# Hybrid Conformer/RWKV-7 trunk on one core: the scheduler's queue order taken from a simulated timeline

## Chip, cores, metric

The kernel runs on one core of one Trainium2 chip. The metric is device time in microseconds of one execution; lower is better. The engines named below are PE (matrix multiply), DVE (vector), ACT (scalar), POOL, and SP, whose queue issues most of the DMAs. Each engine works through its own queue in the order in which the built program lists it.

## Reference

A decoder trunk of 2 layers over 512 tokens of width 1024, with 16 learned tokens put in front (528 rows). All of it is float32. Each layer is: half a SwiGLU feed-forward step, a mixer, half a SwiGLU step, each added to the residual and layer-normalised.

```python
for l in range(DEPTH):
    h = layer_norm(ALPHA*h + 0.5*swiglu(h, ffn1_wg, ffn1_wu, ffn1_wd))
    h = layer_norm(ALPHA*h + mixer(h))
    h = layer_norm(ALPHA*h + 0.5*swiglu(h, ffn2_wg, ffn2_wu, ffn2_wd))

def mixer(x):
    z = x @ w_in                      # glu_a, glu_b, r/k/v and low-rank inputs, two gates
    yc = conv_branch(glu_a, glu_b)    # gated, 31-tap depthwise causal convolution, norm, silu, @ wo
    yr = rwkv_branch(zr)              # time mix, then a scan over tokens per head, group norm, @ wo
    return (sigmoid(gate_c)*yc + sigmoid(gate_r)*yr) @ w_out

def scan_step(S, r, w, k, v, kk, a):  # S is 64x64 for each of 16 heads
    sa = S @ -kk
    S = S*w + outer(sa, kk*a) + outer(v, k)
    return S, S @ r
```

## The kernel before

A float32 product is made of three products of reduced-precision float32 parts: the weight is split into `w_hi` (a cast on ACT, L121 and L123) and `w_lo` (a subtraction on DVE, L132), the activation into a high and a low part (`xh`, `xl`). `wunit` loads a weight tile through SP (L112) and splits it; raw tiles and split tiles have two buffers each in the mixer. Tokens are columns, handled as two halves of 264 (256 in parts of the last layer).

In the feed-forward steps and at the end of a mixer PE streams such products (L185). The mixer is different. Its scan is turned into chunks of 64 tokens, for four groups of four heads (q = 0 to 3):

- `prep(q)` projects k, r and v of a group (token mixing on ACT and DVE, L702 and L704), normalises k (L875, a chain of small DVE operations, L887) and makes the decayed forms.
- `scores(q)`: for each of 8 chunks PE transposes (L986) and multiplies (L995), DVE masks (L1003, L1005), ACT copies; the strictly lower blocks go to DRAM.
- `inverse(q)`: the blocks come back with 16x16 blocks on partitions, and `substitution` solves them in 15 dependent steps of a product (L1028) and a sum (L1032) on DVE. Groups 0 to 2 do it in two lots, so 60 instructions; group 3 in one, 30. The result goes through DRAM into `dd`, and PE joins the blocks (L1074, then three rounds of L1085 with copies between).
- `scan(q)`: 8 chunks, each depending on the last. PE transposes v (L1155), multiplies the state (L1160), ACT copies; PE (L1168, L1170), ACT copies; PE updates the state (L1177), DVE adds and scales it (L1180, L1181), and L1185 makes the output. A step of this sequence is called a link below.
- `post(q)`: group norm of the outputs (L1213 to L1234) and L1279 to L1287.

Work without a place in that chain is called fill. On PE it is the projections of `proj` (L203): 48 matmuls for a 128-column tile, for the two halves of the gated convolution input, the two gates, and k, r and v of later groups. On DVE it is the 31-tap convolution: 30 instructions of L814 for each of 8 tiles, traced at an offset of 4000 towards low priority. The loop interleaves the scan of a group with the scores of the next one, which are traced 50 lower:

```python
for q in range(4):
    scores = self.scores(q + 1, N) if q < 3 else iter(())
    for c, _ in enumerate(self.scan(q, Q)):
        with self.tc.high_priority(offset=-SC_LATE):
            next(scores, None)
        ...
    if q < 3:
        self.inverse(q + 1, N)
    post = early or self.post(q, Q)
    filler(FILL[3][q])
    Q, N = N, prep(q + 2, FILL[4][q]) if q < 2 else None
```

The traced order is only the priority. What stands in a queue is decided when the context closes: a scheduler keeps a clock for each engine, and gives a free engine the instruction of highest priority that its clock says is ready. So the time that the scheduler believes an instruction takes decides how much fill lands between two links. Only `schedule_with_timeline_sim` below is touched; no kernel code says how much fill stands where.

## Time and profile before

| | |
|---|---|
| median of 3 runs | 3326.89 us (3325.49 to 3332.04) |
| profiled execution: its own time | 3317.26 us |
| profiled execution: span of its instructions | 3315.6 us |
| PE busy | 3174.3 us, 96% |
| DVE busy | 1955.1 us, 59% |
| ACT busy | 1228.6 us, 37% |
| mean granted PE clock | 0.952 |

PE executes 27172 matmuls. Busy time of an engine is the time in which it had an instruction at work; the granted clock is 1.00 where PE runs at full rate and 0.50 where the throttle halves it, in which case a busy PE does half as much. The four feed-forward steps take most of the span; the two mixers, without the layer norms ahead of them and the products behind them, lie at 443 to 1125 us and 2101 to 2766 us.

### The profile page before, as it was taken

The page shows a single profiled execution, that of the slowest core. Times are in us where ns is not written, and L with a number is a line of the kernel's source. Part 1 is how long each engine was busy: PE and PEld are TensorE (multiplying, and loading weights), DVE is VectorE, ACT ScalarE, POOL GpSimd, SP SyncE. Part 2 cuts the span into 40 slices and gives each one's busy share as a digit, 9 for nine tenths or more (in the row PEclk, how much of TensorE's full clock was granted, in tenths as well). Part 3 has the DMA queues.
Part 4 walks back from the last instruction along what each step waited for, and adds up shares of the span by engine and source line. Part 5 has one row for each costly group of instructions (what it writes and reads, how often), then busy time and mean ns, then how long its engine had stood idle before and what let it go on. Part 6 is the DMA issues. An engine that isn't in the chain of part 4 may idle for free. (4 is left out here: it accounts for less than half of the span.)

```text
span 3315.6 us, 65004 instructions
## 1 busy us (share of the span) xinstructions
PE 3174.3 (96%) x27172; PEld 3047.5 (92%) x27172; DVE 1955.1 (59%) x4183; ACT 1228.6 (37%) x2477; POOL 19.7 (1%) x89
## 2 busy tenths in 40 slices
PE   9999989899999899999999999889999998999998
PEld 8999979789889899999999999788888898999997
DVE  4343449687788876343363434586688878663434
ACT  4232244334353454322242322534343444342322
POOL 0000000000000000000000000000000000000000
PEclk9999969799899999999999999898898999999999
DMA  5232234222333542332232322432233435432321
GB/s 152 72 107 80 80 113 120 77 75 72 93 106 101 181 135 78 89 109 82 79 96 72 107 82 78 145 97 75 68 96 90 115 89 180 137 90 78 109 82 52
DMA packets 569012, 326.48 MB, mean 98 GB/s; under 512 B 83148, under 2 KB 535104, under 8 KB 568718
## 3 DMA queue, kind: packets, MB, share of 16 engines
q1 hardware_dynamic: 563726, 312.74, 32.8%
q10 hardware_dynamic: 4608, 8.52, 0.7%
q8 instruction: 213, 3.49, 0.4%
q0 software_dynamic: 384, 1.07, 0.1%
q14 instruction: 81, 0.66, 0.1%
HBM read 270.81 MB, written 47.12 MB: 96 GB/s over the span
## 5 line engine op out<-in xcount | busy, mean ns | idle before, releaser
L185 PE MATMUL mm<-xh,w_hi 128*128 128x264 f32 (+1 forms) x2880 | 819.9, 286 | 16.6 <-ACT xh L395 15.8
L185 PE MATMUL mm<-xh,w_lo 128*128 128x264 f32 (+1 forms) x2880 | 821.4, 285 | 0.5 <-DVE w_lo L132 0.5
L185 PE MATMUL mm<-xl,w_hi 128*128 128x264 f32 (+1 forms) x2880 | 819.4, 285 | 0.3 <-DVE xl L396 0.2
L132 DVE TENSOR_TENSOR w_lo<-w_raw,w_hi 128x1024 fp32r<-128x1024 f32 (+3 forms) x540 | 535.0, 993 | 457.8 <-ACT w_hi L123 394.0
L123 ACT CAST w_hi<-w_raw 128x1024 fp32r<-128x1024 f32 (+2 forms) x388 | 372.3, 961 | 770.3 <-PE mm L185 540.1
L185 PEld LDWEIGHTS mm<-xh,w_hi 128*128 128x128 f32 x2880 | 546.4, 190 | 19.7 <-ACT xh L395 17.7
L185 PEld LDWEIGHTS mm<-xh,w_lo 128*128 128x128 f32 x2880 | 547.6, 190 | 0.8 <-DVE w_lo L132 0.8
L185 PEld LDWEIGHTS mm<-xl,w_hi 128*128 128x128 f32 x2880 | 547.1, 190 | 1.2 <-DVE xl L396 1.1
L203 PE MATMUL mm<-xh,w_hi 128*128 128x264 f32 x1760 | 400.2, 305 | 46.8 <-DVE glus L794 17.9
L203 PE MATMUL mm<-xh,w_lo 128*128 128x264 f32 x1760 | 395.7, 304 | 6.6 <-DVE w_lo L132 6.6
L185 PE MATMUL mm<-hl,w_hi 128*128 128x264 f32 (+1 forms) x1408 | 400.5, 284 | 0.0
L185 PE MATMUL mm<-hh,w_hi 128*128 128x264 f32 (+1 forms) x1408 | 400.3, 284 | 0.0
L185 PE MATMUL mm<-hh,w_lo 128*128 128x264 f32 (+1 forms) x1408 | 398.7, 283 | 0.0
L203 PE MATMUL mm<-xl,w_hi 128*128 128x264 f32 x1760 | 397.7, 304 | 0.0
L814 DVE SCALAR_TENSOR_TENSOR cacc<-cu,cw,cacc 128x528 f32<-128x528 f32 (+1 forms) x480 | 362.3, 755 | 9.3 <-ACT cacc L812 2.1
L203 PEld LDWEIGHTS mm<-xh,w_hi 128*128 128x128 f32 x1760 | 297.4, 202 | 55.7 <-issue 30.3
L203 PEld LDWEIGHTS mm<-xh,w_lo 128*128 128x128 f32 x1760 | 293.7, 201 | 13.3 <-DVE w_lo L132 7.1
L203 PEld LDWEIGHTS mm<-xl,w_hi 128*128 128x128 f32 x1760 | 294.9, 201 | 6.9
L443 DVE TENSOR_TENSOR g<-g,mm 128x264 f32<-128x264 f32 (+1 forms) x176 | 74.7, 427 | 330.1 <-PE mm L185 318.4
L185 PEld LDWEIGHTS mm<-hh,w_lo 128*128 128x128 f32 x1408 | 265.1, 188 | 0.1
L185 PEld LDWEIGHTS mm<-hl,w_hi 128*128 128x128 f32 x1408 | 264.9, 188 | 0.2
L185 PEld LDWEIGHTS mm<-hh,w_hi 128*128 128x128 f32 x1408 | 264.6, 188 | 0.1
(340 smaller groups left out, 4517.2 us busy)
## 6 DMA issues: line engine op xcount, KB each, us to landing
w_raw<-in_w_in_dram SPq DMA_DIRECT2D x116, 512.0 KB
w_raw<-in_ffn_wg_dram SPq DMA_DIRECT2D x88, 512.0 KB
w_raw<-in_ffn_wu_dram SPq DMA_DIRECT2D x88, 512.0 KB
w_raw<-in_ffn_wd_dram SPq DMA_DIRECT2D x64, 384.0 KB
w_raw<-in_ffn_wd_dram SPq DMA_DIRECT2D x64, 320.0 KB
w_raw<-in_rwkv_wo_dram SPq DMA_DIRECT2D x16, 512.0 KB
w_raw<-in_conv_wo_dram SPq DMA_DIRECT2D x16, 512.0 KB
w_raw<-in_w_out_dram SPq DMA_DIRECT2D x16, 512.0 KB
```

The lines of the kernel that those rows point to most:

```text
L123: self.nc.scalar.copy(hi[:, :kt], raw[:, :kt])
L132: self.nc.vector.tensor_tensor(lo[:, k], raw[:, k], hi[:, k].bitcast(F32), op=ALU.subtract)
L185: self.nc.tensor.matmul(pm, a[:, k, :], b[:, xk + k, s], start=first and k == 0 and j == 0, stop=last and k == nk - 1 and j == 2)
L203: nc.tensor.matmul(pm[:, h, :n], a[:, wk + k, :], b[:, xk + k, s:s + n], start=first and k == 0 and j == 0, stop=last and k == nk - 1 and ...
L443: nc.vector.tensor_tensor(g, g, ps[1][:, :n], op=ALU.mult)
L814: tap = nc.vector.scalar_tensor_tensor(y, x, w, y, op0=ALU.mult, op1=ALU.add)
```

## The change

The scheduler takes its estimates from a simulated timeline of the machine; before, it used a fixed figure for each instruction.

```diff
-    with tile.TileContext(nc) as tc, ExitStack() as ctx:
+    with tile.TileContext(nc, schedule_with_timeline_sim=True) as tc, ExitStack() as ctx:
         Trunk(ctx, tc, aps, out).run()
```

The same instructions are built, apart from waits: PE has 24276 matrix instructions in both, DVE 4183. ACT has 35 loads of its function tables where it had 31. In the middle of the feed-forward steps the order is the same on all engines; around layer norms a few instructions change places; in the two mixers fill and chain are interleaved in another way. Three places show it.

PE, scan of group 2 in layer 0, between the multiplication of the state (L1160) and the next link (L1168). `sv` is the state, `G` and `FB` the decayed rows, `w` and `va` ACT's copies; L203 is fill. Before:

```order
L1185 MATMUL ch<-va,sb 64x64 x4
L1160 MATMUL tr<-sv,G 64x64 x4
L203 MATMUL mm<-xl,w_hi 128x264 x2
L203 MATMUL mm<-xh,w_lo 128x264
L986 MATMUL sc<-ident,FB 128x128
L1168 MATMUL tr<-w_10566,G 64x64
```

Now:

```order
L1185 MATMUL ch<-va,sb 64x64 x4
L1160 MATMUL tr<-sv,G 64x64 x4
L995 MATMUL sc<-G,FB 128x128 x4
L203 MATMUL mm<-xh,w_hi 128x264
L203 MATMUL mm<-xl,w_hi 128x264 x2
L203 MATMUL mm<-xh,w_lo 128x264 x2
L203 MATMUL mm<-xh,w_hi 128x264 x2
L203 MATMUL mm<-xl,w_hi 128x264 x2
L203 MATMUL mm<-xh,w_lo 128x264 x2
L203 MATMUL mm<-xh,w_hi 128x264 x2
L203 MATMUL mm<-xl,w_hi 128x264 x2
L1168 MATMUL tr<-w_10566,G 64x64
```

Three fill matmuls stood in this link; now 15 do, and in most links of scans 0, 1 and 2 that have fill it is 20 to 25.

PE, scan of group 3 in layer 0, the same link. Before:

```order
L1185 MATMUL ch<-va,sb 64x64 x4
L203 MATMUL mm<-xh,w_lo 128x264 x2
L203 MATMUL mm<-xh,w_hi 128x264 x2
L203 MATMUL mm<-xl,w_hi 128x264
L1160 MATMUL tr<-sv,G 64x64 x4
L203 MATMUL mm<-xl,w_hi 128x264
L203 MATMUL mm<-xh,w_lo 128x264 x2
L203 MATMUL mm<-xh,w_hi 128x264 x2
L1168 MATMUL tr<-w_11598,G 64x64
```

Now:

```order
L1185 MATMUL ch<-va,sb 64x64 x4
L1160 MATMUL tr<-sv,G 64x64 x4
L1168 MATMUL tr<-w_11598,G 64x64
L1170 MATMUL ch<-sv,G 64x64
```

All fill has moved out of this scan, to places ahead of it.

DVE, substitution of group 1 in layer 0. `ix` is the block being solved, `is` a product, `cacc` the convolution's sum. Before:

```order
L1028 TENSOR_TENSOR is<-im,ix 64x55 x2
L1032 TENSOR_TENSOR ix<-ix,is 64x11x5 x2
L1028 TENSOR_TENSOR is<-im,ix 64x60 x2
L1032 TENSOR_TENSOR ix<-ix,is 64x10x6 x2
L1028 TENSOR_TENSOR is<-im,ix 64x63 x2
L1032 TENSOR_TENSOR ix<-ix,is 64x9x7 x2
```

Now:

```order
L1028 TENSOR_TENSOR is<-im,ix 64x55
L814 SCALAR_TENSOR_TENSOR cacc<-cu_4629,cw,cacc 128x528
L1028 TENSOR_TENSOR is<-im,ix 64x55
L1032 TENSOR_TENSOR ix<-ix,is 64x11x5
L814 SCALAR_TENSOR_TENSOR cacc<-cu_4629,cw,cacc 128x528
L1032 TENSOR_TENSOR ix<-ix,is 64x11x5
L1028 TENSOR_TENSOR is<-im,ix 64x60
L814 SCALAR_TENSOR_TENSOR cacc<-cu_4629,cw,cacc 128x528
L1028 TENSOR_TENSOR is<-im,ix 64x60
L1032 TENSOR_TENSOR ix<-ix,is 64x10x6
```

A tap of the convolution now stands between nearly all of these steps.

Counted over the queues of layer 0 between marks of the chain (layer 1 is alike), the fill matmuls L203 on PE and the taps L814 on DVE are:

| Stretch of the mixer (marks on PE) | fill before | fill now | taps before | taps now |
|---|---|---|---|---|
| start: low-rank products to first L986 of scores 0 | 350 | 402 | 22 | 31 |
| scores 0: to their last L995 | 112 | 270 | 8 | 29 |
| substitution 0: to first L1074 | 189 | 0 | 18 | 0 |
| inverse 0 and prep: to first L986 of scores 1 | 119 | 151 | 12 | 4 |
| scan 0 with scores 1: to last L995 | 54 | 360 | 11 | 56 |
| substitution 1 (and the end of scan 0) | 240 | 113 | 19 | 30 |
| inverse 1 and prep: to first L986 of scores 2 | 287 | 127 | 17 | 3 |
| scan 1 with scores 2 | 94 | 257 | 12 | 57 |
| substitution 2 (and the end of scan 1) | 210 | 192 | 11 | 15 |
| inverse 2 and prep: to first L986 of scores 3 | 260 | 126 | 26 | 0 |
| scan 2 with scores 3 | 86 | 575 | 12 | 0 |
| substitution 3 (and the end of scan 2) | 275 | 19 | 30 | 0 |
| inverse 3: to first L1160 of scan 3 | 55 | 0 | 16 | 0 |
| scan 3 | 161 | 0 | 11 | 0 |
| end of the scan to the products behind the mixer | 100 | 0 | 15 | 15 |

## Prediction

> **What bounds the kernel now.** I read the page first, then busy time by stretch, then single waits. The page:
>
> ```profile
> span 3315.6 us, 65004 instructions
> PE 3174.3 (96%) x27172; PEld 3047.5 (92%) x27172; DVE 1955.1 (59%) x4183; ACT 1228.6 (37%) x2477; POOL 19.7 (1%) x89
> PEclk9999969799899999999999999898898999999999
> ```
>
> PE is busy nearly always; only 141 us could be won by closing its waits. The clock dips where the mixers lie. So I cut the first mixer at the marks of its chain (columns: stretch, its length, then busy time of PE, its weight loads, DVE, ACT and POOL, granted clock, DMA share, GB/s); the rows stand in the order of the front table, with the two mixers whole and a feed-forward stretch after them.
>
> ```profile
> 443.00:541.10 98.10, 92.78 (x556) 85.48 (x556) 56.02 (x113) 42.90 (x76) 0.30 (x4) 0.76 0.47 154
> 541.10:564.70 23.60, 23.41 (x199) 20.68 (x199) 22.77 (x75) 12.01 (x33) 0.00 (x0) 1.00 0.48 132
> 564.70:605.50 40.80, 30.47 (x236) 28.83 (x232) 35.44 (x96) 9.28 (x15) 0.85 (x4) 0.87 0.33 77
> 605.50:657.70 52.20, 47.42 (x468) 44.03 (x468) 31.19 (x74) 20.22 (x56) 0.30 (x4) 0.74 0.21 61
> 657.70:697.70 40.00, 39.73 (x464) 32.33 (x462) 28.56 (x90) 23.17 (x69) 0.44 (x2) 1.00 0.18 51
> 697.70:739.20 41.50, 35.23 (x262) 34.55 (x258) 35.64 (x100) 8.09 (x16) 0.42 (x2) 0.88 0.38 93
> 739.20:801.60 62.40, 62.40 (x624) 60.45 (x623) 41.99 (x98) 25.21 (x65) 0.30 (x4) 0.89 0.31 93
> 801.60:849.90 48.30, 48.09 (x503) 38.24 (x499) 37.47 (x128) 27.77 (x76) 0.44 (x2) 1.00 0.30 83
> 849.90:885.10 35.20, 31.05 (x254) 29.84 (x253) 29.77 (x91) 10.40 (x22) 0.42 (x2) 0.95 0.39 100
> 885.10:948.70 63.60, 63.59 (x618) 60.57 (x619) 48.98 (x108) 24.73 (x64) 0.16 (x2) 0.87 0.34 94
> 948.70:992.30 43.60, 43.54 (x471) 35.48 (x469) 34.65 (x123) 25.18 (x71) 0.44 (x2) 1.00 0.34 94
> 992.30:1029.70 37.40, 37.40 (x319) 36.47 (x317) 34.58 (x80) 12.62 (x24) 0.00 (x0) 1.00 0.56 151
> 1029.70:1054.00 24.30, 24.30 (x314) 23.73 (x313) 16.96 (x26) 9.69 (x34) 0.00 (x0) 0.80 0.31 95
> 1054.00:1101.50 47.50, 47.50 (x503) 40.68 (x503) 33.91 (x106) 22.95 (x56) 1.24 (x2) 1.00 0.26 80
> 1101.50:1124.80 23.30, 13.32 (x110) 12.83 (x107) 21.65 (x41) 11.00 (x18) 1.08 (x2) 0.88 0.53 180
> 443.00:1124.80 681.80, 640.24 (x5866) 584.21 (x5865) 509.58 (x1336) 285.22 (x691) 6.38 (x32) 0.89 0.36 102
> 2101.10:2766.30 665.20, 617.87 (x5793) 565.56 (x5792) 499.00 (x1268) 280.33 (x683) 6.22 (x32) 0.91 0.37 104
> 1328.00:1660.00 332.00, 332.00 (x2729) 331.77 (x2728) 125.90 (x200) 93.91 (x157) 0.00 (x0) 1.00 0.31 88
> ```
>
> Three things are to be seen. In the scans (40.0, 48.3, 43.6, 47.5 us) PE is full at full clock: fill just covers the links. In the substitutions (40.8, 41.5, 35.2, 37.4 us) PE has almost nothing but fill, and DVE and the DMAs set the length. And a fill matmul costs 332.0/2729 = 0.1217 us, the price of each one moved into a full stretch.
>
> **The change part by part.** Fill moves forward, from substitutions, inverses, scan 3 and the end, into scores 0 and scans 0 to 2. Work added to a full PE lengthens a stretch; work taken from under a wait shortens nothing.
>
> (a) Scores 0 and the three mixed scans. Added fill by the table is 158, 306, 163 and 489: 19.2, 37.2, 19.8 and 59.5 us, so PE needs 42.8, 77.2, 68.1 and 103.1 us. DVE has taps moved in there as well:
>
> ```profile
> L814 DVE SCALAR_TENSOR_TENSOR cacc<-cu,cw,cacc 128x528 f32<-128x528 f32 x240 | 183.2, 763 | 5.5 <-ACT cacc L812 2.1
> L132 DVE TENSOR_TENSOR w_lo<-w_raw,w_hi 128x512 fp32r<-128x512 f32 x152 | 103.2, 684 | 57.2 <-ACT w_hi L121 40.1 <-ACT G L1089 15.1 <-ACT w L1162 1.5
> ```
>
> Summed instruction by instruction, at the durations of this trace, DVE's queue has 48.7, 78.8, 91.9 and 47.4 us between these marks (of it 29, 56, 57 and 0 taps at 0.763). The larger of PE and DVE: 48.7 + 78.8 + 91.9 + 103.1 = 322.5; in scan 0 the two take turns as the longer from chunk to chunk, which I put at 6 more. 328 against 155.5 us: **+173**. The chain cannot hide it: a link needs much less than 20 fills (2.4 us), as PE's own rows of one chunk of scan 3 show:
>
> ```profile
> 1059.68 0.68 PE L1160 MATMUL tr<-sv,G 128*64 128x64 f32 x8
> 1061.10 0.27 PE L1168 MATMUL tr<-w,G 64*64 64x64 f32 x1
> 1062.39 0.68 PE L1177 MATMUL ch<-va,sb 128*64 128x64 f32 x8
> 1064.88 0.68 PE L1160 MATMUL tr<-sv,G 128*64 128x64 f32 x8
> ```
>
> From the end of L1160 (1060.36) to L1168 it is 0.74 us, with a whole chunk in 5.2 us.
>
> (b) Substitutions. Their bare length is the way to DVE through DRAM, the steps, and the way back. For group 2 (last mask, first step, two pairs of steps, last step on DVE; then PE, which waited for the DMA):
>
> ```profile
> 851.47 0.27 DVE L1005 TENSOR_TENSOR G<-sc,msk 64x128 f32<-64x128 f32 x1
> 857.59 0.16 DVE L1028 TENSOR_TENSOR is<-im,ix 64x15 f32<-64x15 f32 x1
> 865.07 0.47 DVE L1028 TENSOR_TENSOR is<-im,ix 64x60 f32<-64x60 f32 x2
> 865.57 0.46 DVE L1032 TENSOR_TENSOR ix<-ix,is 64x60 f32<-64x60 f32 x2
> 876.96 0.17 DVE L1032 TENSOR_TENSOR ix<-ix,is 64x15 f32<-64x15 f32 x1
> 885.11 1.10 PE L1074 MATMUL sc<-dd,ut 64*64 64x48 f32 x16 [0.95 <-DMA dd<-xdscr]
> ```
>
> Ways in and out take 5.9 + 8.0 us here and up to 20 in group 1, where other work stood in the queues; I take 16, since SP's order around these loads changes too. Thirty pairs at up to 0.50 us make 14.6 us; group 3 has half. Now group 0 has no work between (31 us), group 1 has 29 taps, 5 `w_lo` and 3.1 us of other work between its steps (14.6 + 22.1 + 3.4 + 3.1 + 16 = 59), group 2 has 15 taps, 6 `w_lo` and 7.4 us (53.5), group 3 only 2.1 us (25.5). Sum 169 against 154.9: **+14**. PE's work there (113, 192 and 19 fills, at most 23 us, and some small products) lies inside; what is left is open waiting.
>
> (c) Inverses and preparation lose 317 fills net: -38.6 us if all of it came back. But PE's rows there have a clock of 0.74 to 0.89 even where it is busy throughout, and the copies between rounds, now uncovered, must be waited for. I take half: **-20**.
>
> (d) The start gains 52 fills (+6.3) and loses its 5.3 us of waiting, since 143 fills now stand between L877 and L887, and some time at low clock: **-2**.
>
> (e) Scan 3 runs without fill. It falls back to its chain, 5.2 us a chunk with fill; its three groups of small products run slower at half clock, an estimate of 1.3 us more: 8 x 6.5 = 52 against 47.5. The end was already open waiting (13.3 of 23.3 us busy) and stays: **+4**.
>
> On the clock, the wait at the end of the scan shows what follows one:
>
> ```profile
> 1120.00:1130.00 10.00, 5.24 (x26) 5.24 (x27) 9.82 (x14) 4.44 (x7) 0.00 (x0) 0.53 1.05 385
> 1130.00:1140.00 10.00, 10.00 (x85) 10.00 (x84) 7.49 (x13) 3.17 (x4) 0.00 (x0) 1.00 0.82 245
> ```
>
> PE got 26 matmuls done in 5.24 us, 0.20 each, and 85 in the next ten, 0.118 each. This is the row behind the 1.3 us. The Trainium skill, "TensorE: Matmul & The Clock Gate", Part 1, says that an idle window of about 3.4 us halves the clock and one such window of sustained work restores it. That speaks against this change, which opens such gaps; by it alone, though, scan 3, busy for over half of each chunk, would regain full rate, and (e) would be some 10 us lower for each layer (3647 us in all). The trace agrees on the drop, but the 0.80 of the inverse with PE busy all through says that small products do not bring the clock back, so I keep mine.
>
> The four added table loads of ACT (1.28 us each by this row) are costed at nothing: ACT is 37% busy; without that cover 5 us.
>
> ```profile
> L372 ACT ACT_TABLE_LOAD x10 | 12.8, 1283 | 1.7 <-PEq L1486 0.8 <-ACT glus L827 0.8
> ```
>
> The feed-forward streams keep their order; the layer norms around them exchange a few places, for which I allow 10 us either way and take 0.
>
> Sum for layer 0: 173 + 14 - 20 - 2 + 4 = +169. Layer 1 has the same counts within some ten fills; its start ran at a better clock (its mixer is 16.6 us shorter) and has less to win there, so +171. The profiled execution took 3317.3 us; 3317.3 + 340 = 3657. The median of the runs stands 9.6 us above it: 3667 us.
>
> **The rivals.**
>
> Faster: the fill ahead of each link closes PE's waits, and the order gains what PE lost. The mixers wait 41.6 + 47.3 = 88.9 us, so 3317.3 - 88.9 = 3228 at best, less with a better clock. It decides if the four substitutions (25 to 59 us each) had other PE work; the queue has none for group 0 and 19 fills for group 3. Chance 0.03.
>
> Fill alone counts: DVE's taps never hold the chain. Then (a) is 291 (+136), (b) +6 at worst, (c) -38, the rest -14: +90 for a layer, 3507 on the median. The DVE sums of 92 us for scan 1 and 59 us for substitution 1 speak against. Chance 0.12.
>
> Worse coupling: `w_lo` of the next tile stands on DVE behind a link's step that waits for PE, and PE's fill waits for `w_lo`. The trace has one such wait of length:
>
> ```profile
> PE mm L203 <- DVE w_lo L132: 6.3, 1, 6.3
> ```
>
> Some 31 tiles a layer are fill in the lengthened stretches (1462/48); at half of that wait each, 3 us, it is +93 a layer: 3853. Against it, (a) leaves PE and DVE no slack that would make such waits the rule. Chance 0.10.
>
> No measurable change: only if gains and losses cancel, since the order does differ. Chance 0.02.
>
> **How the numbers follow.** The forecast of 0.73 is 3667. Its own range takes the ends of its terms: (a) 155 to 190, (b) 0 to 35, (c) -38 to 0, (d) and (e) together -10 to 18, about 3560 to 3775 since ends do not fall together. Reaching down to the second rival in part gives 3530 to 3780. Within 0.2% (about what a measurement of this kernel tells from no change) 0.02, faster 0.03, slower 0.95.
>
> **What would show it.** In the new trace: PE full for over 95 us in scan 2 and for some 75 us in scan 0; PE idle for 25 to 30 us ahead of L1074 in groups 0 and 3; taps between L1028 and L1032; scan 3 at 5 to 7 us a chunk with PE half idle; granted clock below 0.952; feed-forward streams unchanged at 0.12 us. Wrong would be: PE's waits not lengthened ahead of L1074, or scans 0 to 2 no longer than before, which would mean that fill there replaced waiting.

## Result, and the profile after

The changed kernel takes 3635.76 us (median of 4 runs, 3631.82 to 3643.28) against 3328.32 us: 1.0936 times as long, 95% interval 1.0906 to 1.0966, or 307 us more. The profiled execution, 3643.28 us, is the longest of the four. Its page:

```profile
span 3641.5 us, 65106 instructions
PE 3274.4 (90%) x27172; PEld 3135.4 (86%) x27172; DVE 1957.6 (54%) x4183; ACT 1231.5 (34%) x2481; POOL 19.6 (1%) x89
PEclk9999978787779589999999999888887885999999
```

The same 27172 matmuls keep PE busy 100 us longer (3174.3 before), and PE is idle 367 us instead of 141. So of the 326 us between the two profiled spans, 100 are the same matmuls taking longer and 226 are waiting. The clock has fallen in both mixers, not between them. The first mixer, cut at the same marks of the chain as before (columns as in the prediction's first table; rows: start, scores 0, substitution 0, inverse 0, then scan, substitution and inverse in turn up to scan 3 and the end), and the two mixers whole:

```profile
457.80:561.30 103.50, 98.50 (x608) 89.46 (x608) 65.68 (x124) 47.89 (x83) 0.30 (x4) 0.80 0.50 159
561.30:613.30 52.00, 48.39 (x399) 45.19 (x398) 42.47 (x102) 18.59 (x39) 0.44 (x2) 0.91 0.33 92
613.30:639.10 25.80, 0.48 (x5) 0.18 (x2) 14.94 (x69) 1.04 (x3) 0.42 (x2) 0.50 0.16 24
639.10:696.60 57.50, 55.11 (x488) 51.85 (x488) 24.56 (x66) 20.87 (x58) 0.30 (x4) 0.68 0.24 67
696.60:775.30 78.70, 75.90 (x738) 68.52 (x737) 69.07 (x149) 32.66 (x84) 0.44 (x2) 0.98 0.27 79
775.30:829.20 53.90, 22.35 (x177) 20.77 (x173) 46.12 (x117) 8.04 (x18) 0.42 (x2) 0.69 0.21 52
829.20:882.70 53.50, 51.12 (x475) 47.56 (x476) 23.62 (x65) 19.45 (x54) 0.30 (x4) 0.71 0.21 58
882.70:961.00 78.30, 70.33 (x618) 60.92 (x617) 70.51 (x176) 31.54 (x81) 0.43 (x2) 0.84 0.33 96
961.00:1010.50 49.50, 34.79 (x270) 32.52 (x269) 41.31 (x110) 12.23 (x27) 0.42 (x2) 0.81 0.23 56
1010.50:1069.30 58.80, 56.46 (x474) 52.91 (x474) 21.17 (x61) 17.61 (x52) 0.16 (x2) 0.62 0.23 59
1069.30:1170.50 101.20, 101.20 (x955) 93.77 (x951) 40.09 (x131) 41.44 (x100) 0.43 (x2) 1.00 0.41 121
1170.50:1193.40 22.90, 7.98 (x83) 6.68 (x79) 11.61 (x42) 4.23 (x11) 0.00 (x0) 0.66 0.47 110
1193.40:1216.70 23.30, 22.55 (x259) 22.09 (x259) 2.20 (x4) 7.76 (x30) 0.00 (x0) 0.50 0.05 6
1216.70:1269.00 52.30, 41.47 (x340) 32.00 (x341) 22.91 (x88) 18.25 (x47) 1.23 (x2) 0.50 0.09 27
1269.00:1282.00 13.00, 1.53 (x9) 0.97 (x7) 10.75 (x28) 6.03 (x11) 1.08 (x2) 0.50 0.42 143
457.80:1282.00 824.20, 688.15 (x5865) 625.39 (x5864) 507.01 (x1326) 287.64 (x693) 6.37 (x32) 0.77 0.30 85
2276.80:3081.10 804.30, 666.87 (x5793) 606.72 (x5792) 494.44 (x1258) 284.22 (x685) 6.20 (x32) 0.79 0.30 86
```

Three shapes: scores 0 and scans 0 to 2 are long and full or nearly so; substitutions 0 and 3 are open waits; what follows a wait (inverses, scan 3) runs at 0.50 to 0.71. The waits of PE, in total, times, longest:

```profile
PE sc L1074 <- DMA dd<-xdscr: 145.0, 8, 30.6
PE mm L185 <- ACT xh L395: 25.6, 5, 6.2
PE mm L185 <- DVE xl L396: 15.7, 7, 3.1
PE mm L185 <- ACT w_hi L123: 12.4, 3, 10.2
```

The first was 1.0 us before, and the one for `xl` 0.2. The mixers grew by 142.4 and 139.1 us. That leaves 44 us outside them (layer norms, products behind the mixers, feed-forward streams): 14.8 ahead of the first mixer, 18.5 between the two, 11.1 behind the second. In the middle of the feed-forward streams nothing has changed (from 1500 to 1600 us PE is busy for all 100 us at a clock of 1.00 in both kernels).

### The profile page after: what moved, and what is told of

It reads as the page before. It is cut to its first block, busy times and chain, and to the rows that moved or that the text cites. A ratio compares the mean times of both kernels' runs of the same rounds, so it can differ in the third digit from the quotient of the medians.

```text
span 3641.5 us, 65106 instructions
## 1 busy us (share of the span) xinstructions
PE 3274.4 (90%) x27172; PEld 3135.4 (86%) x27172; DVE 1957.6 (54%) x4183; ACT 1231.5 (34%) x2481; POOL 19.6 (1%) x89
## 4 chain that ended last, share of the span: by engine, by line
PE 80%; DVE 12%; DMA 3%; ACT 2%; issue 1%; SPq 1%; ACTq 0%; DVEq 0%
PE mm L185 50%; PE mm L203 14%; DVE cacc L814 4%; PE sc L1085 2%; DVE ix L1032 1%; DVE is L1028 1%; PE ch L1177 1%; PE tr L1168 1%; DVE w_lo L132 1%; PE ch L1185 1%; PE tr L1160 1%; PE sc L995 1%; PE ch L1085 1%; PE tr L1085 1%; PE sc L1074 1%
## 5 line engine op out<-in xcount | busy, mean ns | idle before, releaser
L185 PE MATMUL mm<-xl,w_hi 128*128 128x264 f32 (+1 forms) x2880 | 820.4, 285 | 15.7 <-DVE xl L396 15.7
L185 PEld LDWEIGHTS mm<-xh,w_hi 128*128 128x128 f32 x2880 | 544.5, 191 | 40.9 <-ACT xh L395 27.6
L203 PE MATMUL mm<-xh,w_hi 128*128 128x264 f32 x1760 | 390.1, 300 | 30.8 <-DVE G L704 16.4
L203 PE MATMUL mm<-xl,w_hi 128*128 128x264 f32 x1760 | 386.5, 297 | 0.0
L203 PE MATMUL mm<-xh,w_lo 128*128 128x264 f32 x1760 | 383.1, 296 | 1.0 <-DVE w_lo L132 1.0
L814 DVE SCALAR_TENSOR_TENSOR cacc<-cu,cw,cacc 128x528 f32<-128x528 f32 (+1 forms) x480 | 360.4, 751 | 12.2 <-ACT cacc L812 7.7
L203 PEld LDWEIGHTS mm<-xh,w_hi 128*128 128x128 f32 x1760 | 288.8, 197 | 43.5 <-issue 15.2
L203 PEld LDWEIGHTS mm<-xh,w_lo 128*128 128x128 f32 x1760 | 287.0, 196 | 5.9 <-DVE w_lo L132 1.4
L203 PEld LDWEIGHTS mm<-xl,w_hi 128*128 128x128 f32 x1760 | 288.7, 197 | 3.7
L443 DVE TENSOR_TENSOR g<-g,mm 128x264 f32<-128x264 f32 (+1 forms) x176 | 74.8, 427 | 327.1 <-PE mm L185 325.1
```

The source lines that it names most:

```text
L185: self.nc.tensor.matmul(pm, a[:, k, :], b[:, xk + k, s], start=first and k == 0 and j == 0, stop=last and k == nk - 1 and j == 2)
L203: nc.tensor.matmul(pm[:, h, :n], a[:, wk + k, :], b[:, xk + k, s:s + n], start=first and k == 0 and j == 0, stop=last and k == nk - 1 and ...
L443: nc.vector.tensor_tensor(g, g, ps[1][:, :n], op=ALU.mult)
L814: tap = nc.vector.scalar_tensor_tensor(y, x, w, y, op0=ALU.mult, op1=ALU.add)
```

## The experiments

Each was timed beside runs of the kernel before on the same chip; ratios are to that kernel. In the code below, `...` stands for lines left out, `self.scored` is the last product L995 of a group, and `self.nosync(a, b)` puts `a` behind `b` in their queue. Line numbers in an edited kernel can differ by a few; the text uses those of the kernel before.

**e1: fill back under the waits, nothing in the scans.**

```diff
-        self.mac(pm, w, self.x, 0, T // 2, KT)
+        self.mac(pm, w, self.x, 0, T // 2, KT, after=self.pin)  # first matmuls stand behind it
...
-        filler(FILL[1])
+        filler(FILL[1], self.scored)         # self.scored: last L995 of the group
-            filler(FILL[3][q])
+            filler(FILL[3][q], self.scored)
-        filler(2 * KT + 2 * KT)
+        filler(2 * KT + 2 * KT, self.scored)
```

> The changed kernel with the same estimates, but every tile of convolution input and gate that is traced behind a substitution may stand on PE only behind the last score product of that group. On the queues this puts 182 to 205 fill matmuls back into each substitution of layer 0, 298 to 395 into the inverses and preparations, 348 into scan 3, and none into scores 0 and scans 0 to 2. Theory of the forecast (the loss is fill that stands in full stretches and is missing under waits): start 88, scores 0 20, substitutions 28 + 35 + 32 + 27, inverses with preparation 58 + 68 + 59 + 40, scans 48 + 48 + 46 + 62, end 13: 672 us a layer against 824, so about 3635 - 304 = 3330 us. Rival (the clock decides: a scan without fill runs at half clock whatever stands elsewhere): the three scans that now have no fill take some 62 us each, 717 us a layer or more, 3420 us and up. Rival (other parts of the new order, such as loads and layer norms, carry the loss): it stays above 3550 us.

Measured: 3586.42 us, 1.0761 (1.0744 to 1.0778). Only 49 us came back where the theory of the forecast had some 300, and by its own wording the number goes to the last rival, that other parts of the new order carry the loss. The scans shrank as expected (47.1, 53.9 and 43.8 us in layer 0), but some of what gained fill grew by more than was put on it. The stretch ahead of scores 2 and scan 3:

```profile
768.80:868.70 99.90, 88.09 (x754) 82.69 (x754) 79.47 (x151) 31.71 (x76) 0.30 (x4) 0.78 0.30 89
1155.20:1231.50 76.30, 71.31 (x689) 64.31 (x689) 32.75 (x102) 31.02 (x69) 1.23 (x2) 0.95 0.35 105
```

Expected were 68 and 62 us. In the first row DVE is busy 79 us: 63 taps have moved into it. So fill under the waits is not enough; e6 and e10 take this apart.

**e6: the same pins under the fixed estimates.** The edit of e1 with `tile.TileContext(nc)`.

> The same pins as in e1, with the scheduler's fixed estimates instead of the simulated timeline. Fill matmuls on the queue of layer 0: start 288, scores and scans 0 to 2 none, substitutions 209, 239, 235, 333, inverses with preparation 271, 337, 293, 48, scan 3 147, end 192. If the missing fill in the scans made e1 slow, this one is as slow, near 3560 us. If what the new estimates do to the rest of the order (taps, layer norms, start) made it, this one comes out near 3400 us or lower.

Measured: 3412.67 us, 1.0249 (1.0222 to 1.0276). With next to no fill in scans 0 to 2 the old estimates lose 84 us, not 256, so the missing fill in the scans is not what made e1 slow. The stretch that took 99.9 us in e1:

```profile
756.60:824.00 67.40, 66.47 (x674) 64.73 (x673) 45.89 (x103) 28.04 (x69) 0.31 (x4) 0.92 0.32 95
```

It has 337 fill matmuls instead of 395, worth 7 us, and 21 taps instead of 63.

**e10: e1 without taps.** One of the 30 taps of each convolution tile is left, so the convolution is incomplete.

```diff
-                tap = nc.vector.scalar_tensor_tensor(y, x, w, y, op0=ALU.mult, op1=ALU.add)
+                if j == TAPS - 1:                      # taps 1 to 29 left out
+                    tap = nc.vector.scalar_tensor_tensor(y, x, w, y, op0=ALU.mult, op1=ALU.add)
```

> The kernel of e1 with 29 of the 30 taps of each convolution tile left out (the convolution is then not the reference's). e1 took 3586 us, the same pins under the fixed estimates (e6) 3413: 174 us apart, of which e7 puts 44 on the start and the layer norms. Theory that the rest is the taps, which the new estimates crowd into the preparations (63 in front of scores 2 against 21 in e6): about 3586 - 130 = 3455 us. Rival (the clock, or fill crowded into the preparations and scan 3): 3530 to 3586 us.

Measured: 3468.25 us, 1.0415 (1.0392 to 1.0438), 118 us less than e1. The stretch ahead of scores 2, with the same 395 fill matmuls, fell from 99.9 to 79.0 us, and PE is now nearly full in it:

```profile
747.40:826.40 79.00, 78.23 (x715) 77.19 (x715) 36.41 (x86) 28.95 (x70) 0.30 (x4) 0.85 0.34 96
```

So the taps made most of the surplus of e1 (3455 us was expected if so). The 138 us that e10 still loses were not taken apart further. If e7's 44 us can be taken off, some 94 are left, and the same pins alone cost 84 in e6: the pins are themselves a worse order than that of the kernel before, and e1 is no clean undoing of the change.

**e3 and e4: the changed kernel and the kernel before, without taps.** The edit of e10 on each.

> The changed kernel with one of the 30 DVE taps of each convolution tile left (29 are left out, so the convolution is not the reference's); PE's fill stands nearly as in the changed kernel. Theory of the forecast (PE and DVE take turns as the longer; taps stand in the way of substitution steps): scores 0 falls by 9 us to PE's 42.8, scan 0 by 2, scan 1 by 10, substitutions 1 and 2 by 21 and 11: 53 a layer, 3635 - 106 = 3530 us. Rival (fill alone counts, taps never hold the chain): 3625 to 3635 us.

> The kernel before with the same 29 of 30 taps left out. Both theories: PE is the limit there and DVE 59% busy, so little: 3300 to 3330 us. If it falls by over 50 us, taps cost the kernel before as well and the difference to the changed kernel without taps is what the order of the taps adds.

Measured: 3523.99 us, 1.0583 (1.0559 to 1.0607), and 3304.51 us, 0.9897 (0.9851 to 0.9943). Without the taps the changed kernel is 112 us faster and the kernel before 26; by this difference the new order of the taps is worth some 86 of the 307 us. It is a rough figure. The fill moves when taps go: in e4 the end of the mixer has 225 fill matmuls instead of 100 and takes 37.2 us instead of 23.3 (39.6 instead of 24.8 in layer 1), some 29 us that hide a part of what the taps cost the kernel before:

```profile
1078.10:1115.30 37.20, 28.19 (x232) 27.98 (x231) 16.35 (x36) 14.27 (x24) 1.08 (x2) 0.91 0.54 173
```

Where e3 got it back (scan 0, substitution 1, scan 1, substitution 2):

```profile
687.60:763.80 76.20, 74.20 (x743) 67.54 (x741) 34.66 (x97) 33.61 (x86) 0.44 (x2) 1.00 0.30 89
763.80:794.10 30.30, 20.95 (x171) 19.43 (x169) 23.12 (x84) 7.36 (x16) 0.42 (x2) 0.82 0.27 57
853.10:918.20 65.10, 57.53 (x585) 50.37 (x584) 34.69 (x122) 32.25 (x83) 0.44 (x2) 1.00 0.36 107
918.20:957.70 39.50, 30.02 (x240) 27.67 (x240) 26.30 (x87) 10.55 (x24) 0.41 (x2) 0.83 0.26 53
```

Scan 0 loses 2.5 us (2 expected), since PE's fill is as long there as DVE's taps; scan 1 loses 13.2 (10), substitution 1 23.6 (21), substitution 2 10.0 (11). The 9 us that were expected in scores 0 did not come (52.5 us against 52.0): PE was the longer there, and 29 more fill matmuls stand in it. The rival that fill alone counts (3625 to 3635 us) falls.

**e5: fill pulled forward, by the old scheduler.**

```diff
+            def between(c, link):
+                filler(1 + c % 2, link)        # behind L1160 of chunk c
+                return self.tile               # its last matmul; L1168 stands behind that
...
-            for c, _ in enumerate(self.scan(q, Q)):
+            for c, _ in enumerate(self.scan(q, Q, between if q == 2 else None)):
...
-            filler(FILL[3][q])
+            filler(FILL[3][q] if q < 2 else 0)
```

> The kernel before, its own scheduler, with one thing of the change alone: in scan 2, 12 tiles of gates and convolution input are tied behind L1160 of a chunk (one or two in turn) and L1168 waits for them. On the queue scan 2 then has 544 fill matmuls instead of 86 (575 in the changed kernel), substitution 3 has 128, inverse 3, scan 3 and the end have none; all ahead of scan 2 is as before. Theory of the forecast (placing alone makes the loss): scan 2 some 97 us, substitution 3 26, inverse 3 23, scan 3 52, end 13: 211 against 176 us in layer 0, about +70 in all, 3400 us. Rival (the loss comes with other parts of the new order): 3330 us within 15.

Measured: 3428.58 us, 1.0283 (1.0251 to 1.0316): 99 us more, from one scan in each layer (70 expected). Scan 2 and substitution 3 of layer 0, and the start of layer 1:

```profile
945.20:1054.90 109.70, 104.34 (x980) 94.05 (x978) 91.73 (x206) 43.52 (x106) 0.43 (x2) 1.00 0.40 122
1054.90:1077.20 22.30, 15.98 (x131) 15.78 (x130) 10.73 (x38) 5.80 (x10) 0.00 (x0) 0.96 0.49 115
2142.90:2239.20 96.30, 90.95 (x553) 83.59 (x553) 55.64 (x113) 42.58 (x75) 0.30 (x4) 0.77 0.48 156
```

The five stretches from scan 2 to the end take 213.8 us in layer 0 (211 expected, 176 before). The mixers grew by 34 and 59 us, and 16 us more came outside them; 15 of the 59 lie in the third row, whose queue is that of before (81.6 us there, at 0.94). That row is taken up in e12. So the placing of fill, by the old scheduler, makes a loss in the mixers at about the price put on it: 78 us without that row. It is not PE's fill alone that moved: the taps of its tiles came along (67 start in scan 2 of layer 0 instead of 11), though PE, busy 104.3 of 109.7 us, was the longer there.

**e7: the edges outside the mixers.**

```diff
-        extra = [(4 + 4 * l, lambda mm, l=l: self.layer_vectors(l, self.room, mm)) for l in range(DEPTH)]
+        def vectors(l, mm):
+            with self.tc.issue_after(self.wload.ins):     # the latest weight load on SP
+                self.layer_vectors(l, self.room, mm)
+        extra = [(4 + 4 * l, lambda mm, l=l: vectors(l, mm)) for l in range(DEPTH)]
...
+            if len(lows) > 1:                  # lows: the L396 of this layer norm so far
+                self.nosync(scaled, lows[-2])  # scaled: L385 of this slice
```

> The changed kernel with two edits outside the mixers: the loads of the layer vectors stand on SP behind the first eight weight tiles, and in a layer norm the scaling of slice o + 2 stands behind the subtraction of slice o on DVE, as the kernel before has it by itself. Fill in the mixers stays within a few matmuls. The trace of the changed kernel shows 14 us lost at the start and some 30 us at the other edges. Theory that these two orders make them: the start gives back 13 us, the norms 3 us each at some seven places, 3600 us. Rival (the edges wait for something else): 3620 to 3636 us.

Measured: 3592.04 us, 1.0792 (1.0771 to 1.0812): 44 us less. DVE's rows at one layer norm of the changed kernel show what the second edit undoes:

```profile
1442.00 3.31 DVE L385 SCALAR_TENSOR_TENSOR a<-a,vec,ln_rstd 128x264 f32<-128x264 f32 x8
1445.23 1.32 DVE L374 TENSOR_TENSOR ln_sq<-ln_sq 128x528 f32<-128x528 f32 x2
1446.47 3.31 DVE L396 SCALAR_TENSOR_TENSOR xl<-a,vec,xh 128x264 fp32r<-128x264 f32 x8
```

All eight scalings stand ahead of the first subtraction, and PE's first product with `xl` waited 2.1 us here; there are seven such waits, of 1.7 to 3.1 us, 15.7 in all. With the edit the mixers begin at 441.4 us (457.8 in the changed kernel), and 32 of the 44 us outside the mixers are gone; another 19 of the 51 us between the two profiled spans came inside the mixers, where a few fill matmuls changed places. The two edits were made together, so they are not priced apart. What is left outside, some 12 us, includes 10 us of a longer wait for `xh` (26.0 us; 15.8 in the kernel before).

**e2 and e9: spare work under the waits.** In e9 the first L1074 also stands behind the last spare.

```diff
+        if q in (0, 3):                        # e9: all groups, 185, 200, 90 and 120
+            for i in range(200):               # the first stands behind self.scored
+                nc.tensor.matmul(spare[:, :T // 2], xh[:, 0, :P], xh[:, 0, :T // 2], start=True, stop=True)
```

> The changed kernel with 200 spare matmuls (128x264, results unused) on PE behind the last scores of groups 0 and 3, where PE waits 23 to 26 us for the solved blocks; 4 x 24 us of PE work under a wait, nothing on the path. Theory that only the placing of fill and taps counts: no change, 3635 us within 10. Theory that idle PE costs clock: the inverse behind these waits ran at 0.50 and took 24.5 us; at the 0.80 that the kernel before had there, less its fill, some 18 us, so 4 x 6 = 24 us less, 3612 us. If the wait is what lowers the clock for the whole stretch behind it, preparation 0 and scan 3 gain as well, 3580 us or lower.

> The changed kernel with spare matmuls (128x264, results unused) under the wait of all four substitutions, 185, 200, 90 and 120 of them, sized not to outlast the wait, ahead of the first L1074. In e2 the inverse behind such cover ran at 0.80 and took 15.7 us instead of 23.2. If idle PE in the substitutions is what lowers the clock for the inverses: 8 x 7.5 = 60 us less than 3636, 3576 us. If groups 1 and 2 lose their clock elsewhere: 4 x 7.5 = 30 us less, 3606 us. If only placing counts: 3636 us.

Measured: 3626.99 us, 1.0878 (1.0855 to 1.0901), and 3641.19 us, 1.0924 (1.0906 to 1.0941). By the totals neither differs from the changed kernel by more than the 10 us of "only placing counts". Stretch by stretch, e2 shows the clock theory at work at the place it names (substitution 3, inverse 3, scan 3):

```profile
1158.00:1189.50 31.50, 31.50 (x281) 30.16 (x278) 11.60 (x42) 6.45 (x14) 0.00 (x0) 1.00 0.38 84
1189.50:1205.20 15.70, 14.98 (x259) 14.49 (x258) 2.20 (x4) 5.59 (x26) 0.00 (x0) 0.80 0.01 2
1205.20:1257.50 52.30, 41.51 (x340) 32.05 (x341) 22.84 (x88) 18.25 (x47) 1.23 (x2) 0.50 0.09 27
```

The same 259 matmuls take 15.7 us instead of 23.3, but the spares outlast the wait by 8.6 us in this group and eat the gain. Behind substitution 0, where they ended in time, the stretch took 49.7 us instead of 57.5, 2 us of it for 17 fewer fill matmuls. Scan 3 gained nothing. In e9 they were made to end early, and the gain went: inverse 3 of layer 0 takes 20.3 us, and that of layer 1 23.2. Around the first L1074 of groups 0 and 3 in e9:

```profile
635.00:639.00 4.00, 0.00 (x0) 0.00 (x0) 0.00 (x0) 0.62 (x1) 0.42 (x2) 1.00 0.40 85
639.00:641.00 2.00, 0.56 (x6) 0.59 (x6) 0.00 (x0) 0.00 (x0) 0.00 (x0) 0.69 0.65 61
1194.00:1196.00 2.00, 2.00 (x38) 2.00 (x36) 1.23 (x3) 1.02 (x2) 0.00 (x0) 1.00 0.10 9
1198.00:1212.00 14.00, 14.00 (x174) 13.74 (x172) 0.00 (x0) 4.67 (x23) 0.00 (x0) 0.50 0.00 1
```

In group 0 the clock fell in a remaining wait of about 5 us. In group 3 PE waited 1.2 us, and the clock fell 3.5 us after the first small product; in e2, with no wait ahead of them, it fell after some 9. Whether the short wait made the difference was not tested.

**e8 and e11: two tries at a better kernel before.** e8 puts 50 spare matmuls into substitutions 0 to 2 and 75 behind the mixer, e11 raises two evacuations:

```diff
+        if q < 3:                                   # e8, in inverse(q)
+            self.spare(50, self.scored)
...
+        self.spare(75, self.turned)                 # e8, behind the mixer's last transposition
...
+        with self.tc.high_priority(offset=400):     # e11: L794, and the two operations of token_mix
             nc.vector.scalar_tensor_tensor(self.tv(self.glu_s), self.tv(self.glu_s), 1.0,
                                            self.pv(pa), op0=ALU.add, op1=ALU.mult)
```

> The kernel before with 50 spare matmuls (results unused) on PE in substitutions 0 to 2 and 75 behind the mixer's last transposition, where its PE waits 6 to 10 us at a time. Theory that idle PE costs clock: the inverse behind substitution 0 ran at 0.74 and takes some 5 us less, the product behind the mixer 2 us less: 3300 to 3315 us. Theory that only placing counts: 3330 us, or up to 36 more where the spare work delays fill.

> The kernel before with the two evacuations that its PE waits for longest inside the mixers (L794 and L704 on DVE, 18 and 28 us) raised by 400 in priority. If they stood late in DVE's queue only because of their place in the trace, up to 40 us of the waits go: 3290 to 3320 us. If they stood where the scheduler believed them ready, nothing changes but noise of the order: 3330 us within 15.

Measured: 3348.91 us, 1.0056 (1.0034 to 1.0078), and 3328.04 us, 0.9985 (0.9966 to 1.0004). The spares delay more than they speed up, which goes to "only placing counts" (up to 36 us more); scan 0 goes from 40.0 to 44.5 us. The priority changes nothing that can be measured.

**e12: ten spare matmuls in each mixer, in a wait of 1.04 us.** In the trace of before the first low-rank products of layer 0 look like this (2 us to a row, and the stretch from the fall of the clock to its return):

```profile
442.00:444.00 2.00, 2.00 (x17) 1.67 (x15) 1.76 (x3) 1.16 (x3) 0.00 (x0) 1.00 0.00 0
444.00:446.00 2.00, 0.95 (x6) 0.74 (x6) 1.20 (x1) 1.99 (x3) 0.00 (x0) 1.00 0.77 206
446.00:448.00 2.00, 2.00 (x11) 1.73 (x10) 0.65 (x2) 0.96 (x3) 0.00 (x0) 0.69 0.89 327
448.00:450.00 2.00, 2.00 (x8) 1.65 (x8) 0.55 (x2) 0.48 (x1) 0.00 (x0) 0.50 0.52 199
446.70:484.30 37.60, 37.60 (x147) 33.32 (x147) 8.05 (x17) 15.13 (x31) 0.00 (x0) 0.50 0.51 190
```

A short wait, and then 8 low-rank matmuls in 2 us: the clock stays at 0.50 for 37.6 us in which PE is busy all through. Layer 1 has the same wait, 1.04 us on the same queue, and kept its clock there in the kernel before; in e5 it lost it.

```diff
                     m = nc.tensor.matmul(pm, w[a][r, o, :], x[b][r, s], start=j == 0, stop=j == 2)
+                    if act is None and o == 0 and h == 1 and j == 1:
+                        self.spare(10, m)      # behind m, results unused
```

> The kernel before with ten spare matmuls (128x264, results unused) among the first low-rank products of each mixer (L753), where PE waits 1.04 us. In the trace of before the clock falls to 0.50 behind this wait in layer 0 (start of the mixer 98.1 us) and stays at 1.00 in layer 1 (81.6 us) with the same queue. If the wait decides and covering it holds the clock: both starts 82 us, 16 us less than the profiled execution of before, a median of 3305 to 3315 us. If the low-rank products themselves let the clock fall, whatever stands in the gap: 3330 to 3335 us.

Measured: 3286.17 us, 0.988 (0.9843 to 0.9918), faster than both kernels, and by more than the theory had (3305 to 3315 us, 82 us for each start). The same four rows, and the two starts whole (98.1 us at 0.76 and 81.6 at 0.94 before):

```profile
442.00:444.00 2.00, 2.00 (x18) 1.86 (x17) 1.72 (x2) 1.16 (x3) 0.00 (x0) 1.00 0.01 4
444.00:446.00 2.00, 2.00 (x17) 1.82 (x16) 1.44 (x2) 1.97 (x3) 0.00 (x0) 1.00 0.55 153
446.00:448.00 2.00, 2.00 (x15) 1.71 (x14) 0.87 (x2) 1.31 (x4) 0.00 (x0) 1.00 1.03 344
448.00:450.00 2.00, 2.00 (x16) 1.71 (x14) 0.86 (x3) 0.88 (x3) 0.00 (x0) 1.00 0.75 192
443.40:519.80 76.40, 75.05 (x568) 70.48 (x568) 51.69 (x108) 40.37 (x76) 0.30 (x4) 0.98 0.62 198
2074.80:2149.60 74.80, 73.06 (x564) 68.49 (x564) 51.25 (x108) 39.86 (x74) 0.31 (x4) 1.00 0.63 201
```

Where 8 matmuls went in 2 us now 16 go. The starts give 22 and 7 us of the 32 us between the two profiled spans; nearly all else stands as it stood. The medians are 43 us apart, as if layer 1 lost its clock too in most executions of the kernel before; its profiled one, at 3317, is one of the faster. Whether the spares help because they fill the wait, or because they are full-sized products among smaller ones, was not separated.

## Why the prediction was right, and where not

The forecast was 340 us more than the profiled execution of before; the medians are 307 apart, the profiled spans 326. By its own terms, from the rows above and those of before, in us (layer 1 at the same marks):

| Term | forecast, layer 0 | measured, layer 0 | measured, layer 1 |
|---|---|---|---|
| (a) scores 0, scans 0 to 2 | +173 | +154.7 | +148.3 |
| (b) substitutions | +14 | -2.8 | -10.3 |
| (c) inverses, preparation | -20 | -9.4 | -7.9 |
| (d) start | -2 | +5.4 | +17.1 |
| (e) scan 3, end | +4 | -5.5 | -8.2 |
| mixer | +169 | +142.4 | +139.1 |

- **(a)** holds the loss. Scan 2 took 101.2 us (103.1 forecast), full on PE, as said. For the other three the sums of DVE were too long. Such a sum adds up durations, and successive instructions overlap: between PE's marks of scan 1 the durations in the new trace add up to 79.7 us, while DVE is busy 70.5. The rest of the 91.9 is work between marks of DVE's own queue that runs on past PE's. Scan 1 took 78.3 us. Scan 0 took 78.7, next to DVE's sum of 78.8, but that is luck: DVE is busy 69.1 us there and PE 75.9, and without taps it still takes 76.2 (e3). In scores 0 (52.0 us, 48.7 forecast) PE was the longer as well, 48.4 us at a clock of 0.91 against 42.5 of DVE. Taps did lengthen scan 1, by 13.2 us by e3. The 6 us for taking turns were not needed.
- **(b)** was mis-sized by the ways through DRAM: substitution 0, with nothing between, took 25.8 us, not 31, which makes in and out 11 us, not 16. All four come out 3 to 5 us shorter than forecast. Taps between the steps cost about what was put on them (23.6 us in substitution 1 by e3, 22.1 forecast). The sum near nothing hides large parts: substitutions 1 and 2 grew by 12.4 and 14.3 us, 0 and 3 shrank by 15.0 and 14.5. So the fill and taps of before had held up these two waits; without taps but with fill they took 35.6 and 26.7 us (e4; 40.8 and 37.4 before), so both had a part.
- **(c)** Half of what left these stretches was too much to take off. Inverse 3 without any fill took 23.3 us, as long as with 55 fill matmuls before (24.3), because its clock fell from 0.80 to 0.50. e2 shows that it is the clock: 15.7 us at a mean of 0.80 with the wait covered. The prediction read the low clock of these rows as a reason to take half, but not that opening the waits would lower it further.
- **(d)** start: no gain; the clock stayed at 0.80 and 0.83. In layer 1 the start of the kernel before had kept its clock (0.94, 81.6 us), so +17.
- **(e)** Scan 3 took 52.3 us (52 forecast), and the end fell to 13.0 from 23.3, which I had left as it was; none of the 100 fill matmuls that lengthened it is left there. That PE would be half idle in scan 3 was wrong: it is busy 41.5 of 52.3 us, at half clock. That the clock would halve there was right.
- **Outside the mixers** the forecast had 0, within 10 either way, and 44 came. The failed step is "the layer norms around them exchange a few places": eight scalings ahead of the first subtraction are a few places, and they cost PE 1.7 to 3.1 us each time, 15.7 in all; at the start it was SP's queue, with the loads of the vectors ahead of later weight tiles, and a wait of PE of 10.2 us for `w_hi`. Counting changed places did not tell who waits for them. e7 shows 32 of the 44.

The signs that the prediction named were there (PE full for 101.2 us in scan 2 and 75.9 in scan 0, taps between the steps, a clock of 0.886), but for one more: PE's idle time in substitution 3 was 15 us, not 25 to 30, since the last chunk and 19 fill matmuls stand in that stretch.

So the total came close in part by luck, because two errors ran against each other: the mixers were 58 us too dear, the edges 44 us too cheap. The rival "fill alone counts" falls: e3 takes 112 us off the changed kernel, and e3 and e4 together give the order of the taps some 86 us. "Worse coupling" did not show: PE's wait for `w_lo` in fill is 1.0 us in all.

On the clock, the prediction weighed the Trainium skill, "TensorE: Matmul & The Clock Gate", Part 1: an idle window of some 3.4 us halves the clock and one such window of sustained work restores it. By that alone scan 3 would have regained full rate. It stayed at 0.50 for 52.3 us with PE busy 79% of it, and in e9 for 14 us with PE busy 14.00 of them. The first half of the rule agrees with e9, where the clock fell in a wait of about 5 us, but here it also fell behind 1.04 us (e12's rows of the kernel before). The second half does not agree for products as small as these, nor for the low-rank ones, which kept PE busy for 37.60 us at 0.50. In scan 3 of e9 the clock did come back twice (1220.0 to 1223.4 and 1243.9 to 1247.3 us) and fell again.

The 307 us are thus, roughly: 44 outside the mixers (32 of them undone by e7), some 86 for the order of the taps (e3 against e4), and a rest of some 177. The rest was not measured by itself. It is put down to fill in stretches that were full and missing under waits, because e5 makes 78 us in the mixers with one scan of each; the direct undoing, e1, gave back only 49. The shares overlap: slower clock is in all of them. What in the new estimates moves fill ahead of the links was not tried; it stays open.

## What to carry to other kernels

Count, for each stretch that waits and each that is full, what a new order takes away and adds, on every engine that works there: work added to a full stretch costs its whole duration, work taken from under a wait buys only as much as it had held up there (some 29 us in substitutions 0 and 3 of layer 0, where scan 2 alone grew by 58). Read the edges too, by asking who waits for the first result of each group. And look at the granted clock behind each short wait of PE: ten matmuls in each mixer whose result nobody reads were worth 1.2% here, where 450 of them in long waits cost 0.6%.

## What the runs showed of the hardware

- Behind a wait of 1.04 us among low-rank products (weights of 64 or 128 rows, 264 columns) the clock fell to 0.50 and stayed there for 37.6 us with PE busy all through. It does not fall each time: with one queue, the start of a mixer took 98.1 us in layer 0 and 81.6 in layer 1 of the kernel before, 98.0 and 96.3 in e5. With ten spare matmuls in the wait it took 76.4 and 74.8.
- Small products (64x64 by 48 columns or fewer) kept the full clock for some 9 us after large ones (e2: a mean of 0.80 over 15.7 us is 9.4 us at 1.00 and the rest at 0.50) and then lost it with PE busy all through. In e9 they did not win it back in 14 us with PE busy 14.00 of them.
- Small matmuls at half clock make a busy PE: inverse 3, 97% busy in the changed kernel, was 7.6 us longer than in e2, where the clock held for longer.
